# A hybrid decoder layer on one Trainium2 core: low parts of weight tiles made on VectorE in place of GpSimd, and one set of modulation shifts summed by TensorE

## The chip, the core and the metric

The kernel runs on one core of a Trainium2 chip. The core has five engines, each with an instruction queue of its own that it works through in order: TensorE (PE in the profile, with its weight loads as PEld), VectorE (DVE), ScalarE (ACT), GpSimd (POOL) and SyncE (SP, which here issues DMA transfers). The metric is device time in microseconds (us), the median over runs; less is better.

## The reference, cut to what matters

One layer for T = 512 tokens of width D = 2048, all in float32: a conditioned RMSNorm, a mixer of two groups of heads (attention with latent projections, and gated linear attention), a second conditioned RMSNorm, and a feed-forward part that picks 16 of 16,384 single-neuron experts for each token and head.

```python
c_act = silu(c)
mod = c_act @ ada_w + ada_b                       # 2048 x 12288 matrix, one vector
sh1, sc1, g1, sh2, sc2, g2 = split(mod, 6)        # shift, scale, gate, twice
h = rmsnorm(x, mix_norm_g) * (1 + sc1) + sh1
x = x + g1 * hybrid_mixer(h, ...)                 # begins with proj = h @ w_in
h = rmsnorm(x, ffn_norm_g) * (1 + sc2) + sh2
q = (h @ w_q).reshape(B, S, 8, 2, 128)            # 8 heads, 2 halves
s = einsum('bshpd,hpkd->bshpk', q, sub_keys)      # 128 keys each
top_s, top_i = top_k(s, 16)
cand = top_s[0] + top_s[1]                        # sums of pairs
best_s, best_c = top_k(cand, 16)                  # expert ids, then gates
x = x + g2 * experts(h, ids, gates)
return rmsnorm(x, final_norm_g)
```

## The kernel before

Every matrix product of float32 weights is made of three products: a weight tile is split into a high part and the rest, `whi` and `wlo`, the activations into `hhi` and `hlo` (or `h2hi`, `h2lo`), and `mm3` (L107 to 110) adds `whi·hhi`, `whi·hlo` and `wlo·hhi` in PSUM. `load_w` (L265) brings a tile by a DMA on SyncE's queue into `wraw` (five buffers in the first phase, four later) and calls `split` (L112): ScalarE copies the tile to `whi` (L115), and VectorE or GpSimd subtracts it to give `wlo` (L117). Which of the two it is, is the argument `lo_eng`.

The modulation vector is made by `mod_col` (L231). `mod_acc` brings `ada_w` in tiles of 128 x 512 elements (`adaw`, six buffers, DMA on SyncE at L222); VectorE multiplies each row by its entry of silu(c) (`cact`) and accumulates into `acc` (L226 for the first, L228 for the rest). TensorE then sums the 128 rows by a product with a column of ones (L238), and VectorE adds the bias (L240). An `adaw` tile holds four row groups of 128 columns, or one of 384 or 512: here a block of three columns of 128 takes 16 tiles of 128 x 384.

The stages that matter here, with their time in the profiled execution:

- **Start, 0 to 60 us.** Row norms of x. GpSimd scales all 16 tiles of x (L209) while VectorE makes scale A and shift B of the first block of rows (sections 1 and 0 of the modulation, by turns through `both`).
- **Blocks, 60 to 257 us.** The loop over `KBLOCKS` (L296): five blocks of 3, 3, 3, 4 and 3 tiles of 128 rows of h. For each block ScalarE makes `hhi` (L302, L303), VectorE makes `hlo` (L304), and 15 weight tiles are multiplied (L307) and added up (L314 on ScalarE in the first block, L316 on VectorE later). Between weight tiles `advance(3)` works on the modulation of the next block.
- **Gates and values, 257 to 455 us.** `gr` (L427) and `gv` (L433): 64 weight tiles of 128 x 512, with the rest of the modulation on VectorE beside them.
- **Mixer and the second norm, 455 to 907 us.** Untouched by the change, up to `h2lo` (L735) at its end.
- **Retrieval, 907 to 1104 us.** For 16 pairs of a head and a half, `w_q` tiles of 128 x 1024 (L781), products with the keys (L789), then on VectorE `top16` (L765: MAX8, FIND_INDEX8 and MATCH_REPLACE8), sums of pairs (L799), a second `top16`, and the expert ids by a one-hot compare (L820) and reduction (L826). The first expert products (`product1`, L835) fill in, with six weight tiles of their own.
- **The rest, 1104 to 3153 us.** Gates, dense expert products and the last norm. `wlo` is made on VectorE there before and after.

The order of instructions on each engine is set at build time by a scheduler that goes by the program's dependencies and its own costs; the text of the program gives it the priorities.

Of the kernel before, what the change touches and what calls it, by code (L numbers as in the profile page):

```python
# [16 lines left out]
OP = mybir.AluOpType  # L17
# [4 lines left out]
P = 128  # L22
T = 512
TB = 4
D = 2048
KD = 16
# [26 lines left out]
KBLOCKS = ((0, 3), (3, 3), (6, 3), (9, 4), (13, 3))  # L53
# [33 lines left out]
def hybrid_layer(ctx, tc, a, out):  # L87
    nc = tc.nc
# [12 lines left out]
    def bank(tag):  # L101
        return cur[tag][0].tile([P, 512], F32, name="b_" + tag, tag=tag)

    mm = nc.tensor.matmul
# [23 lines left out]
    vec = {}  # L128
# [3 lines left out]
    cact = const.tile([P, KD], F32, name="cact")  # L132
    nc.scalar.activation(cact, vec["c_t"], AF.Sigmoid)
    nc.vector.tensor_tensor(out=cact, in0=cact, in1=vec["c_t"], op=OP.mult)
    A1 = const.tile([P, KD], F32, name="A1")
    B1 = const.tile([P, KD], F32, name="B1")
# [77 lines left out]
    def ada_tile(pool):  # L214
        return pool.tile([P, 512], F32, name="adaw", tag="adaw", bufs=NADA)
# [16 lines left out]
    def mod_col(pool, sec, dst, c0, width):  # L232
        for acc in mod_acc(pool, sec, c0, width):
            yield
        b = bank("m")
        n0, nn = c0 // P, width // P
        for n in range(nn):
            mm(b[:, n:n + 1], acc[:, n * P:(n + 1) * P], ones, start=True, stop=True)  # L238
        d = dst[:, n0:n0 + nn]
        nc.vector.tensor_tensor(out=d, in0=b[:, :nn], in1=vec["ada_b_t"][:, sec * KD + n0:sec * KD + n0 + nn],  # L240
                                op=OP.add)
        if sec in (1, 4):
            g = vec["mixg"] if sec == 1 else vec["ffng"]
            nc.vector.scalar_tensor_tensor(out=d, in0=d, scalar=1.0, in1=g[:, n0:n0 + nn], op0=OP.add, op1=OP.mult)

    def mod_both(pool, c0, width):
        for acc in mod_acc(pool, 5, c0, width):
            yield
        brow = ada_tile(pool)
        nc.sync.dma_start(out=brow[0:1, :], in_=a["ada_b"][:, 5 * D + c0:5 * D + c0 + width])  # L250
        yield
        b = bank("m")
        n0, nn = c0 // P, width // P
        for n in range(nn):
            mm(b[:, n:n + 1], acc[:, n * P:(n + 1) * P], ones, start=True, stop=True)
        nc.vector.tensor_tensor(out=G2[:, n0:n0 + nn], in0=b[:, :nn],
                                in1=vec["ada_b_t"][:, 5 * KD + n0:5 * KD + n0 + nn], op=OP.add)
        b = bank("m")
        mm(b[0:1, :], ones, acc, start=True, stop=False)
        mm(b[0:1, :], ones[0:1, :], brow[0:1, :], start=False, stop=True)  # L260
        nc.scalar.copy(out=acc[0:1, :], in_=b[0:1, :])
        nc.sync.dma_start(out=g2d[:, c0:c0 + width], in_=acc[0:1, :])


    def load_w(pool, src, shape, lo_eng="vector"):  # L265
        raw = pool.tile(shape, F32, name="wraw", tag="wraw", bufs=5 if pool is wp else NWRAW)
        nc.sync.dma_start(out=raw, in_=src)
        return split(pool, raw, shape, "whi", "wlo", lo_eng=lo_eng)
# [6 lines left out]
    def both(*gens):  # L275
        gens = list(gens)
        while gens:
            for g in list(gens):
                try:
                    yield next(g)  # L280
                except StopIteration:
                    gens.remove(g)
# [9 lines left out]
    def first_mods(k0, n):  # L292
        return both(*(mod_col(ada, sec, dst, k0 * P, n * P) for sec, dst in ((1, A1), (0, B1))))

    late = first_mods(*KBLOCKS[0])
    for ib, (k0, n) in enumerate(KBLOCKS):  # L296
        for _ in late:
            pass
        late = first_mods(*KBLOCKS[ib + 1]) if ib + 1 < len(KBLOCKS) else iter(())
        for k in range(k0, k0 + n):  # L300
            t = xT[:, k, :]
            nc.scalar.activation(t, t, AF.Copy, scale=A1[:, k:k + 1])  # L302
            nc.scalar.activation(hhi[k], t, AF.Identity, bias=B1[:, k:k + 1])  # L303
            nc.vector.scalar_tensor_tensor(out=hlo[k], in0=t, scalar=B1[:, k:k + 1], in1=hhi[k],  # L304
                                           op0=OP.add, op1=OP.subtract)
        for i, dst in enumerate(dsts):
            src, m = (a["w_misc"], 80) if dst is None else (a["w_feat"][i - (i > 6)], P)  # L307
            wh, wl = load_w(wp, src[:, k0:k0 + n, :], [P, n, m], "gpsimd")
            b = bank("pj")
            for j in range(n):  # L310
                mm3(b[:m, :], wh[:, j, :], wl[:, j, :], hhi[k0 + j], hlo[k0 + j], j == 0, j == n - 1)
            for d, p in ((dst, b),) if dst is not None else ((kpe0, b[0:64, :]), (glr, b[64:80, :])):
                if ib == 0:
                    nc.scalar.copy(out=d, in_=p)  # L314
                else:
                    nc.vector.tensor_tensor(out=d, in0=p, in1=d, op=OP.add)  # L316
            advance(3)
# [24 lines left out]
    def proj_tile(pool, src, m, xh, xl, nk, evac, half=4, lo_eng="vector"):  # L342
        b = bank("pj")
        for k0 in range(0, nk, half):
            wh, wl = load_w(pool, src[:, k0:k0 + half, :], [P, half, m], lo_eng)
            for j in range(half):
                k = k0 + j
                mm3(b[:m, :], wh[:, j, :], wl[:, j, :], xh[k], xl[k], k == 0, k == nk - 1)
        evac(b)
# [4 lines left out]
    def gr_evac(i):  # L354
        def f(b):
            nc.scalar.activation(gr[:, i, :], b, AF.Sigmoid)
            nc.vector.tensor_tensor(out=gr[:, i, :], in0=b, in1=gr[:, i, :], op=OP.mult)
        return f
# [66 lines left out]
        nc.scalar.activation(cosT, ang, AF.Sin)  # L425

    for i in range(8):  # L427
        proj_tile(wp, a["w_feat"][14 + i], P, hhi, hlo, KD, gr_evac(i), lo_eng="gpsimd")
        early(i)
        advance(10)  # L430
    ckh, ckl, cqh, cql = [h[i:j] for i, j in ((0, 2), (2, 6)) for h in (hhi, hlo)]
    latents = [ckv[:, i, :] for i in range(2)] + [cq[:, i, :] for i in range(4)]
    for half in range(2):  # L433
        bs = [bank("pj") for _ in range(TB)]
        for k in range(KD):
            wh, wl = load_w(wp, a["w_gv"][half, k], [P, 512], "gpsimd")
            for tb in range(TB):
                tsl = slice(tb * P, (tb + 1) * P)
                mm3(bs[tb], hhi[k][:, tsl], hlo[k][:, tsl], wh, wl, k == 0, k == KD - 1)
            advance(2)  # L440
            if (half, k) == (0, 8):
                gates()
            if (half, k) == (0, 0):
                rotary()
            if half == 1 and k >= NLAT and latents:
                i, src = k - NLAT, latents.pop(0)
                nc.scalar.copy(out=hhi[i], in_=src)
                nc.vector.tensor_tensor(out=hlo[i], in0=src, in1=hhi[i], op=OP.subtract)
        for tb in range(TB):
            nc.scalar.copy(out=gv[:, tb, half * 512:(half + 1) * 512], in_=bs[tb])  # L450
# [58 lines left out]
    for part in range(4):  # L509
# [3 lines left out]
        for tb in range(TB):  # L513
            tsl = slice(tb * P, (tb + 1) * P)
            b = bank("up")
# [256 lines left out]
    for h in range(8):  # L772
        tv = rp.tile([P, 2, TB, 16], F32, name="tv", tag="tv")
        ti = rp.tile([P, 2, TB, 16], U32, name="ti", tag="ti")
        for p2 in range(2):
            f = h * 2 + p2
            q = rp.tile([P, T], F32, name="pq", tag="pq")
            b = bank("pj")
            b4 = b.rearrange("p (a b) -> p a b", a=NG)
            for k0 in range(0, KD, 8):  # L780
                wh, wl = load_w(ws, a["w_q"][f][:, k0:k0 + 8, :], [P, 8, P], "gpsimd")  # L781
                for j in range(8):
                    k = k0 + j
                    mm3(b4, wh[:, j, :], wl[:, j, :], h2[0][:, :, k, :], h2[1][:, :, k, :], k == 0, k == KD - 1)
            nc.scalar.copy(out=q, in_=b)
            b = bank("sk")
            for tb in range(TB):
                tsl = slice(tb * P, (tb + 1) * P)
                mm(b[:, tsl], q[:, tsl], keys[:, f, :], start=True, stop=True)  # L789
            sc = rp.tile([P, TB, P], F32, name="sc", tag="sc")  # L790
            nc.scalar.copy(out=sc, in_=b.rearrange("p (a b) -> p a b", a=TB))
            sc2 = rp.tile([P, TB, P], F32, name="sc2", tag="sc2")
            for tb in range(TB):
                top16(tv[:, p2, tb, :], ti[:, p2, tb, :], sc[:, tb, :], sc2[:, tb, :])
# [64 lines left out]
    def next1(lo_eng="vector"):  # L859
        if done1[0] - max(gated[0], NHOST) >= RAW:  # L860
            return
        j = next(todo1, None)
        if j is not None:
            for _ in product1(j, lo_eng):
                pass
            done1[0] += 1

    for _ in range(NPRE - 1):
        next1("gpsimd")
    before_exp = last_gelu[0]  # L870
    next1("gpsimd")
    nc.vector.tensor_tensor(out=gates, in0=bv, in1=bv[:, :, :, 0:1].broadcast_to([P, TB, 8, 16]), op=OP.subtract)
    after(nc.scalar.activation(gates, gates, AF.Exp), before_exp, ORDER)
    sm = rp.tile([P, TB, 8], F32, name="sm", bufs=1)
# [412 lines left out]
```

## Time and profile before

| | |
|---|---|
| median of three runs | 3154.25 us (3148.91, 3154.25, 3155.24) |
| the profiled execution, its own time | 3154.82 us |
| its span in the trace | 3153.1 us, so 1.7 us lie outside it |
| busy: PE, DVE, ACT, POOL | 96%, 81%, 35%, 26% of the span |
| mean granted TensorE clock | 0.988 |

The busy shares are means over all stages. A granted clock of 1.00 is TensorE's upper level of 2.4 GHz, and a lower mean says that part of the stretch ran at 1.2 GHz. A wait is idle time of an engine, put down to the instruction or transfer that ended it. In rows of the timeline, neighbouring instructions overlap by some 0.07 us on VectorE, so the step from one start to the next is what an instruction costs in a full queue.

### The profile page before, as it was taken

How to read it: one execution, taken by the hardware profiler on the slowest of the kernel's cores; microseconds unless marked ns; L12 is line 12 of the kernel's file. 1: busy time of each engine (PE TensorE's matmuls, PEld its weight loads, DVE VectorE, ACT ScalarE, POOL GpSimd, SP SyncE). 2: the span in 40 equal slices, each digit the busy share in tenths (PEclk: the TensorE clock that was granted, in tenths of full speed). 3: DMA queues.
4: the chain of work that ended last, by engine and by line, in shares of the span. 5: the costliest groups of instructions: out<-in, count | busy, mean ns of one | idle time of the engine just before them, and what ended most of it. 6: DMA issues, size and time to landing. Idle time of an engine off the chain costs nothing.

```text
span 3153.1 us, 46222 instructions
## 1 busy us (share of the span) xinstructions
PE 3037.6 (96%) x17617; PEld 2808.5 (89%) x17617; DVE 2563.7 (81%) x3676; ACT 1111.5 (35%) x1604; POOL 835.0 (26%) x596
## 2 busy tenths in 40 slices
PE   3988999999999999999999999999999999999997
PEld 2777777667777899999999999999999999999997
DVE  8988966677489998688888888888888888888885
ACT  3333344432232355433333333333333333333333
POOL 6445430111233300122222222222222222222210
PEclk9999998999999999999999999999999999999999
DMA  6876943038632257999999999999999999999983
GB/s 219 275 239 197 313 150 101 28 111 287 209 130 85 88 208 262 323 331 350 336 336 335 342 341 337 343 343 333 341 344 335 343 338 340 339 344 338 352 296 121
DMA packets 268527, 850.02 MB, mean 270 GB/s; under 512 B 25768, under 2 KB 99528, under 8 KB 224560
## 3 DMA queue, kind: packets, MB, share of 16 engines
q1 hardware_dynamic: 221712, 511.38, 47.4%
q0 software_dynamic: 46592, 335.68, 28.4%
q8 instruction: 138, 2.26, 0.3%
q14 instruction: 85, 0.70, 0.1%
HBM read 814.74 MB, written 32.19 MB: 269 GB/s over the span
## 4 chain that ended last, share of the span: by engine, by line
PE 84%; DVE 10%; DMA 2%; issue 2%; ACT 1%; SPq 0%; POOL 0%; ACTq 0%; DVEq 0%; POOLq 0%
PE b_p L1080 31%; PE b_p L844 21%; PE b_p L847 10%; PE b_o L703 3%; PE b_pj L109 2%; PE b_pj L110 2%; PE b_pj L108 2%; DVE acc L228 2%; PE b_gg L967 1%; DMA adaw<-in_ada_w 1%; PE b_o L108 1%; PE b_o L109 1%; PE b_o L110 1%; DVE oh L820 1%; PE b_sc L560 1%
## 5 line engine op out<-in xcount | busy, mean ns | idle before, releaser
L115 ACT CAST whi<-wraw 128x1024 fp32r<-128x1024 f32 (+2 forms) x459 | 414.2, 905 | 1036.3 <-PE b_p L844 338.4
L844 PE MATMUL b_p<-h2hi,whi 128*128 128x352 f32 x2048 | 671.4, 328 | 0.0
L844 PE MATMUL b_p<-h2lo,whi 128*128 128x352 f32 x2048 | 666.3, 326 | 0.0
L1080 PE MATMUL b_p<-h2hi,whi 128*128 128x352 f32 x2048 | 655.2, 323 | 0.6 <-DVE xo L1092 0.6
L1080 PE MATMUL b_p<-h2lo,whi 128*128 128x352 f32 x2048 | 653.8, 322 | 0.0
L1074 ACT CAST whi<-wraw 128x1024 fp32r<-128x1024 f32 x256 | 268.7, 1050 | 640.8 <-PE b_p L1080 326.5
L1075 DVE TENSOR_TENSOR wlo<-wraw,whi 128x1024 fp32r<-128x1024 f32 x256 | 312.7, 1223 | 159.6 <-ACT whi L1074 130.0
L117 DVE TENSOR_TENSOR wlo<-wraw,whi 128x1024 fp32r<-128x1024 f32 x282 | 345.0, 1224 | 65.1 <-ACT whi L115 62.0
L844 PEld LDWEIGHTS b_p<-h2lo,whi 128*128 128x128 f32 x2048 | 385.8, 188 | 0.1
L1080 PEld LDWEIGHTS b_p<-h2hi,whi 128*128 128x128 f32 x2048 | 384.4, 188 | 1.4 <-DVE xo L1092 0.9
L844 PEld LDWEIGHTS b_p<-h2hi,whi 128*128 128x128 f32 x2048 | 385.5, 188 | 0.0
L1080 PEld LDWEIGHTS b_p<-h2lo,whi 128*128 128x128 f32 x2048 | 384.9, 188 | 0.0
L228 DVE SCALAR_TENSOR_TENSOR acc<-adaw,cact,acc 128x512 f32<-128x512 f32 (+1 forms) x390 | 356.2, 932 | 29.9 <-DMA adaw<-in_ada_w 24.3
L847 PE MATMUL b_p<-h2hi,wlo 128*128 128x352 f32 x2048 | 377.9, 327 | 0.0
L1080 PE MATMUL b_p<-h2hi,wlo 128*128 128x352 f32 x2048 | 369.8, 322 | 0.0
L117 POOL TENSOR_TENSOR wlo<-wraw,whi 128x512 fp32r<-128x512 f32 (+4 forms) x177 | 277.6, 1576 | 344.5 <-ACT whi L115 333.4
L847 PEld LDWEIGHTS b_p<-h2hi,wlo 128*128 128x128 f32 x2048 | 339.1, 188 | 0.0
L1080 PEld LDWEIGHTS b_p<-h2hi,wlo 128*128 128x128 f32 x2048 | 334.0, 188 | 0.0
L995 POOL DMA_INDIRECT gat<-in_u_rows,eidx x128 | 188.3, 1471 | 510.5 <-ACT whi L1074 201.6
L995 POOL DMA_INDIRECT gat<-in_v_rows,eidx x128 | 185.5, 1449 | 515.6 <-ACT whi L1074 227.8
L1014 DVE SCALAR_TENSOR_TENSOR h2sb<-gat,wt,h2sb 128x2048 f32<-128x2048 f32 x127 | 297.9, 2346 | 26.9 <-DMA gat<-in_v_rows,eidx 26.4
L1001 DVE SCALAR_TENSOR_TENSOR gat<-gat,h2s 128x2048 f32<-128x2048 f32 x128 | 290.8, 2284 | 20.1 <-DMA gat<-in_u_rows,eidx 18.5
(375 smaller groups left out, 4194.1 us busy)
## 6 DMA issues: line engine op xcount, KB each, us to landing
wraw<-in_u_t SPq DMA_DIRECT2D x256, 512.0 KB
wraw<-in_v_t SPq DMA_DIRECT2D x256, 512.0 KB
adaw<-in_ada_w SPq DMA_DIRECT2D x288, 256.0 KB
adaw<-in_ada_w SPq DMA_DIRECT2D x128, 192.0 KB
gd<-stg SPq DMA_DIRECT2D x11, 2048.0 KB
gtile<-gd SPq DMA_DIRECT2D x32, 704.0 KB
wraw<-in_w_out SPq DMA_DIRECT2D x32, 512.0 KB
wraw<-in_w_q SPq DMA_DIRECT2D x32, 512.0 KB
```

Of the source, the lines that this page charges most:

```text
L108: mm(o, wh, xh, start=first, stop=False)
L115: nc.scalar.copy(out=hi, in_=src)
L117: last_lo[0] = e.tensor_tensor(out=lo, in0=src, in1=hi, op=OP.subtract).ins.name
L228: nc.vector.scalar_tensor_tensor(out=acc, in0=w[:, j, :], scalar=cact[:, k:k + 1], in1=acc, op0=OP.mult, op1=OP.add)
L844: mm(b3, uh[:, kk, :], x[:, GA:, k0 + kk, :], start=k0 + kk == 0 and x is h2[0], stop=False)
L847: mm(b3, ul[:, kk, :], h2[0][:, GA:, k0 + kk, :], start=False, stop=k0 + kk == KD - 1)
L995: ins = nc.gpsimd.indirect_dma_start(out=g, out_offset=None, in_=a[table], in_offset=bass.IndirectOffsetOnAxis(ap=idx[:, c:c + 1], axis=0))
L1001: after(nc.vector.scalar_tensor_tensor(out=g, in0=g, scalar=1.0, in1=of(s, h2s, h2sb)[0], op0=OP.mult, op1=OP.mult, accum_out=act0[:, s:s ...
L1014: ins = nc.vector.scalar_tensor_tensor(out=acc, in0=g, scalar=wt0[:, s:s + 1], in1=acc, op0=OP.mult, op1=OP.add)
L1074: pace[0] = nc.scalar.copy(out=vh, in_=vr).ins.name
L1075: pace[1] = nc.vector.tensor_tensor(out=vl, in0=vr, in1=vh, op=OP.subtract).ins.name
L1080: mm(banks[dc][:, :NT], part[:, jj, dc * P:(dc + 1) * P], x, start=first and jj == 0 and part is vh and x is wpair[pair * 2 + jj][0], stop ...
```

## The change

The argument "gpsimd" goes from four calls of `load_w` and `proj_tile` and from the first three `next1`, so that VectorE makes all their `wlo`: 75 tiles in the blocks, 32 in `gr`, 32 in `gv`, 32 in retrieval and 6 in the first expert products. And the shift B of the first block comes from a new function, in which TensorE multiplies the `adaw` tiles with `cact` itself: 16 tiles, three products of 128 x 128 by 128 x 1 each, summed in one bank of PSUM, and one addition on VectorE at the end.

```diff
+    def mod_pe(pool, sec, dst, c0, width):
+        b = bank("m")
+        n, kn = width // P, 512 // width
+        for k0 in range(0, KD, kn):
+            w = ada_tile(pool)[:, :kn * width].rearrange("p (k n) -> p k n", k=kn)
+            nc.sync.dma_start(out=w, in_=ada_v[:, k0:k0 + kn, sec * D + c0:sec * D + c0 + width])
+            for j in range(kn):
+                for i in range(n):
+                    mm(b[:, i:i + 1], w[:, j, i * P:(i + 1) * P], cact[:, k0 + j:k0 + j + 1],
+                       start=k0 + j + i == 0, stop=k0 + j == KD - 1 and i == n - 1)
+            yield
+        i0 = sec * KD + c0 // P
+        nc.vector.tensor_tensor(out=dst[:, c0 // P:c0 // P + n], in0=b[:, :n], in1=vec["ada_b_t"][:, i0:i0 + n], op=OP.add)
...
-    late = first_mods(*KBLOCKS[0])
+    late = both(mod_col(ada, 1, A1, 0, KBLOCKS[0][1] * P), mod_pe(ada, 0, B1, 0, KBLOCKS[0][1] * P))
...
-            wh, wl = load_w(wp, src[:, k0:k0 + n, :], [P, n, m], "gpsimd")
+            wh, wl = load_w(wp, src[:, k0:k0 + n, :], [P, n, m])
...
-        proj_tile(wp, a["w_feat"][14 + i], P, hhi, hlo, KD, gr_evac(i), lo_eng="gpsimd")
+        proj_tile(wp, a["w_feat"][14 + i], P, hhi, hlo, KD, gr_evac(i))
...
-            wh, wl = load_w(wp, a["w_gv"][half, k], [P, 512], "gpsimd")
+            wh, wl = load_w(wp, a["w_gv"][half, k], [P, 512])
...
-                wh, wl = load_w(ws, a["w_q"][f][:, k0:k0 + 8, :], [P, 8, P], "gpsimd")
+                wh, wl = load_w(ws, a["w_q"][f][:, k0:k0 + 8, :], [P, 8, P])
...
     for _ in range(NPRE - 1):
-        next1("gpsimd")
+        next1()
     before_exp = last_gelu[0]
-    next1("gpsimd")
+    next1()
```

All lines of the changed program behind the new function stand 14 further down (L304 becomes L318, L766 becomes L780). The build moves instructions; three places show how.

TensorE's queue at the start, the difference: L156 is the last product of the norm, L254 the new products, L238 the sums over rows, L108 to 110 the first weight tiles of the first block.

```order
 L156 MATMUL b_m<-ident,stat 128x128 x4
-L238 MATMUL b_m<-ones,acc 128x1 x6
-L108 MATMUL b_pj<-h0hi,whi 128x512 x2
+L254 MATMUL b_m<-cact,adaw 128x1 x48
+L238 MATMUL b_m<-ones,acc 128x1 x3
+L108 MATMUL b_pj<-h0hi,whi 128x512 x4
 L109 MATMUL b_pj<-h0lo,whi 128x512
 L110 MATMUL b_pj<-h0hi,wlo 128x512
```

The 48 new products stand between the norm's and the three sums of A; the three sums of B are gone.

VectorE's queue at the same place, the difference: L228 accumulates the modulation, L240 and L258 add the bias to A and B, L117 makes `wlo`.

```order
 L228 SCALAR_TENSOR_TENSOR acc<-adaw,cact,acc 128x384
 L151 TENSOR_TENSOR stat<-stat 128x4
-L228 SCALAR_TENSOR_TENSOR acc<-adaw,cact,acc 128x384 x21
+L117 TENSOR_TENSOR wlo<-wraw,whi 128x384 x3
+L228 SCALAR_TENSOR_TENSOR acc<-adaw,cact,acc 128x384 x11
+L258 TENSOR_TENSOR B_91<-b_m,v_ada_b_t 128x3
 L240 TENSOR_TENSOR A_90<-b_m,v_ada_b_t 128x3
```

Behind the last step of the norm (L151), 11 accumulations are left of 21, and three `wlo` stand ahead of them (a fourth stands two rows higher).

VectorE's queue where retrieval begins, before: L735 makes `h2lo`, L766 is the first MAX8 of the first `top16`.

```order
L731 SCALAR_TENSOR_TENSOR h2t<-x1T,A_92,b_m 128x512
L735 SCALAR_TENSOR_TENSOR h2lo<-h2t,B_93,h2hi 128x16x32 x2
L766 MAX tv<-sc 128x8 x2
L767 MAX_INDEX ti<-tv,sc 128x8
L768 MATCH_REPLACE sc_7532<-tv,sc 128x128
```

The same place after, and behind it the piece some 35 rows on at the sums of pairs of head 0 (L813, before L799).

```order
L745 SCALAR_TENSOR_TENSOR h2t<-x1T,A_92,b_m 128x512
L749 SCALAR_TENSOR_TENSOR h2lo<-h2t,B_93,h2hi 128x16x32
L117 TENSOR_TENSOR wlo<-wraw,whi 128x1024
L749 SCALAR_TENSOR_TENSOR h2lo<-h2t,B_93,h2hi 128x16x32
L117 TENSOR_TENSOR wlo<-wraw,whi 128x1024 x3
L780 MAX tv<-sc 128x8 x2
...
L813 TENSOR_TENSOR cd<-tv 128x4x48
L783 MAX tv<-sc_7651 128x8
L117 TENSOR_TENSOR wlo<-wraw,whi 128x1024
L784 MAX_INDEX ti<-tv,sc_7651 128x8
L813 TENSOR_TENSOR cd<-tv 128x4x64
```

Of the 38 `wlo` of 128 x 1024 that come to VectorE, seven stand ahead of the first MAX8 (three of them still further up than these rows), and 31 stand between the steps of retrieval, about four to a head, in the one queue that also holds `top16`.

## Rows read from the trace of the kernel before

**Rows 1.** Busy time by stretch (us): PE, PEld, DVE, ACT, POOL; PEclk; DMA share; GB/s.

```profile
58.00:257.00 199.00, 182.41 (x777) 142.25 (x778) 175.65 (x243) 70.98 (x130) 97.94 (x80) 0.97 0.82 257
257.00:455.00 198.00, 191.57 (x864) 156.63 (x863) 159.62 (x178) 71.06 (x111) 92.54 (x64) 0.97 0.64 211
907.00:1104.00 197.00, 194.02 (x923) 159.57 (x922) 194.24 (x897) 57.29 (x74) 74.00 (x31) 1.00 0.26 87
```

**Rows 2.** Chain of waits over the retrieval, 907 to 1104 us, by line.

```profile
by line: DVE oh L820 12.1%; DVE ti L770 9.3%; DVE ids L826 9.2%; DVE ti L767 8.6%; DVE sc L768 8.5%; DVE cd L799 6.6%; DVE tv L769 6.6%; DVE tv L766 6.4%; DVE oh L823 4.9%; DVE place L770 4.4%; DVE cd L768 4.0%; DVE place L767 4.0%; DVE pla
```

**Rows 3.** Timeline of GpSimd, then of VectorE, in head 0: start, length, what.

```profile
917.04 2.36 POOL L117 TENSOR_TENSOR wlo<-wraw,whi 128x1024 fp32r<-128x1024 f32 x1 [3.31 <-ACT whi L115]
...
916.42 0.35 DVE L799 TENSOR_TENSOR cd<-tv 128x192 f32<-128x192 f32 x1
...
917.29 2.40 DVE L799 TENSOR_TENSOR cd<-tv 128x256 f32<-128x256 f32 x1
```

**Rows 4.** Waits of TensorE, 58 to 257 us: total, times, longest.

```profile
PE b_m L238 <- DVE acc L228: 6.0, 2, 5.5
PE b_pj L110 <- POOL wlo L117: 5.2, 9, 1.7
```

**Rows 5.** Wait of TensorE, 880 to 1112 us.

```profile
PE b_pj L109 <- DVE h2lo L735: 1.8, 1, 1.8
```

**Rows 6.** Timeline of the start: TensorE (two rows), VectorE, GpSimd.

```profile
29.80 2.05 PE L156 MATMUL b_m<-ident,stat 128*128 128x128 f32 x8 [5.94 <-DVE stat L151]
...
55.87 2.95 PE L238 MATMUL b_m<-ones,acc 128*128 128x1 f32 x12 [24.02 <-DVE acc L228]
...
32.71 24.55 DVE L228 SCALAR_TENSOR_TENSOR acc<-adaw,cact,acc 128x384 f32<-128x384 f32 x16 [0.41 <-DMA adaw<-in_ada_w]
...
32.55 24.30 POOL L209 TENSOR_TENSOR xT<-xT,rr 128x512 f32<-128x512 f32 x16 [4.78 <-ACT rr L206]
```

**Rows 7.** Lines by shape, VectorE then GpSimd, 58 to 257 us: busy, mean ns.

```profile
L228 DVE SCALAR_TENSOR_TENSOR acc<-adaw,cact,acc 128x384 f32<-128x384 f32 x90 | 68.3, 808 | 5.0 <-DMA adaw<-in_ada_w 4.8
...
L228 DVE SCALAR_TENSOR_TENSOR acc<-adaw,cact,acc 128x512 f32<-128x512 f32 x56 | 52.9, 965 | 1.1 <-DMA adaw<-in_ada_w 0.7
...
L304 DVE SCALAR_TENSOR_TENSOR h1lo<-xT,B,h1hi 128x512 fp32r<-128x512 f32 x10 | 10.6, 1090 | 0.0
...
L117 POOL TENSOR_TENSOR wlo<-wraw,whi 128x384 fp32r<-128x384 f32 x54 | 64.9, 1213 | 66.6 <-ACT whi L115 64.8 <-PE b_pj L109 1.8
...
L117 POOL TENSOR_TENSOR wlo<-wraw,whi 128x512 fp32r<-128x512 f32 x17 | 24.1, 1428 | 28.4 <-ACT whi L115 28.4
```

**Rows 8.** The tile adaw over the whole span: ns min/median/max.

```profile
L228 DVE SCALAR_TENSOR_TENSOR acc<-adaw,cact,acc x390: 596/752/1864, 20.7 to 820.3; 128x512 f32<-128x512 f32 x135, 128x384 f32<-128x384 f32 x60
```

**Rows 9.** Lines by shape, VectorE, 257 to 455 us.

```profile
L228 DVE SCALAR_TENSOR_TENSOR acc<-adaw,cact,acc 128x512 f32<-128x512 f32 x95 | 109.6, 1154 | 3.4 <-DMA adaw<-in_ada_w 0.6
```

**Rows 10.** Lines by shape, VectorE, 907 to 1104 us.

```profile
L820 DVE TENSOR_TENSOR oh<-pick,iota 128x1024 bf16<-128x1024 bf16 x16 | 25.2, 1574 | 0.0
...
L799 DVE TENSOR_TENSOR cd<-tv 128x192 f32<-128x192 f32 x8 | 7.5, 940 | 0.0
...
L806 DVE TENSOR_SCALAR place<-place 128x64 uint32<-128x64 uint32 x16 | 6.9, 472 | 0.2
...
L799 DVE TENSOR_TENSOR cd<-tv 128x256 f32<-128x256 f32 x8 | 6.8, 853 | 0.0
```

**Rows 11.** Two lines by source, 907 to 1104 us: ns min/median/max.

```profile
L820 DVE TENSOR_TENSOR oh<-pick,iota x16: 676/686/2772, 927.2 to 1101.5; 128x1024 bf16<-128x1024 bf16 x16
...
L806 DVE TENSOR_SCALAR place<-place x16: 179/188/1271, 924.9 to 1098.0; 128x64 uint32<-128x64 uint32 x16
```

**Rows 12.** Timeline of VectorE at low parts that it makes before, two places.

```profile
1114.80 1.22 DVE L117 TENSOR_TENSOR wlo<-wraw,whi 128x1024 fp32r<-128x1024 f32 x1
...
1115.93 0.68 DVE L955 TENSOR_TENSOR o<-iota,slot 128x1024 f16<-128x1024 f16 x1
...
469.19 0.68 DVE L117 TENSOR_TENSOR ulo<-uraw,uhi 128x512 fp32r<-128x512 f32 x1
```

## The prediction

> **What bounds the kernel now.** I read the busy time by stretch first, since the shares of the whole span say nothing of a single stage [rows 1]. From 1104 us on the program is the same before and after, so the end moves by what the stages up to there gain or lose. In the blocks (58 to 257 us) TensorE is busy 182.4 of 199 us, VectorE 175.7, GpSimd 97.9. In the gates and values (198 us) TensorE has 191.6, VectorE 159.6, GpSimd 92.5. In retrieval (197 us) VectorE has 194.2 and TensorE 194.0, so both are full, and the chain of waits there names VectorE alone, one-hot compare (L820) first [rows 2].
>
> Then I looked at why VectorE's instructions take so long where GpSimd works beside them. In head 0 GpSimd's subtraction for a `wlo` of 128 x 1024 runs from 917.04 to 919.40 us; a sum of pairs (L799) on VectorE begins at 917.29 and ends at 919.69, 2.40 us for 256 elements a row, where one of 192 elements just before took 0.35 [rows 3]. So some instructions of VectorE stand still until GpSimd's ends. The compare at L820 shows the same: 0.69 us at the median, 2.77 at most; L806 0.19 and 1.27 [rows 11]. The Trainium skill, page "SBUF — State Buffer", section "Who interferes with whom", says that VectorE's second pair of ports is GpSimd's only one, held as an exclusive lock by whichever uses it; the trace agrees with the 2.40 us beside 0.35. By that rule the whole excess goes when GpSimd falls silent, as in the sum below; without it the same sum would have 27 us more in retrieval.
>
> Last I read what TensorE waits for. In the blocks the largest are 6.0 us for the modulation's accumulation (one wait of 5.5) and 5.2 us in nine waits for a `wlo` of GpSimd [rows 4]. Ahead of retrieval there is one of 1.8 us for `h2lo` [rows 5].
>
> **The start.** TensorE ends the norm's spread at 31.85 us and then waits 24.0 us for VectorE's accumulation [rows 6]. VectorE runs 16 accumulations there in 24.55 us, 1.53 each, beside GpSimd's 16 scalings in 24.30. The change takes the shift's 16 accumulations from VectorE and gives TensorE 48 products. The nearest row is the sums at L238, of the same shape (128 x 128 by 128 x 1): 12 instructions for six calls in 2.95 us, 0.246 each. So 48 calls are 96 instructions, 23.6 us, and they stand behind the norm in the queue: 31.85 + 23.6 = 55.5, and three sums of A (six instructions, 1.5 us) end at 57.0. On VectorE 11 accumulations and three or four `wlo` at 1.53 each, since GpSimd's scaling still runs, take 21 to 23 us from 32.7 on, so its end is 54 to 56 us, too. Before, the sums of A were done at 57.3 and those of B at 58.8. TensorE's wait is thus filled with work of nearly the same length: **0**. The bounds: if the products took no time the start would come at VectorE's 55 + 1.5, hardly a gain; without the lock VectorE's 14 or 15 instructions of about 0.6 would be through some 14 us sooner, but then TensorE's 23.6 hold. If a product costs 0.2 instead of 0.246 and the accumulations slip between the scalings, some 4 to 6 us are gained. To lose, the transfers have to be late: a `wlo` now stands in VectorE's queue ahead of accumulations and waits for ScalarE's copy and the tile's DMA, and the shift's tiles hold `adaw` buffers until TensorE is past the norm. The same queue showed 0.41 us of waiting for transfers [rows 6], so I bound this by +3.
>
> **The blocks.** GpSimd loses 54 `wlo` of 128 x 384, 17 of 128 x 512 and five smaller ones in this stretch [rows 7]. On VectorE a `wlo` of 128 x 1024 lasts 1.22 us and the next instruction starts 1.13 after it; one of 128 x 512 lasts 0.68, so its step is about 0.60 [rows 12]; in a line between them 128 x 384 is 0.47 (an estimate). That is 25.4 + 10.2 + 1.7 = 37.3 us more. What VectorE gets back: the accumulation's lowest and median durations over all are 0.596 (384) and 0.752 (512) [rows 8], against means of 0.808 x 90 and 0.965 x 56 here [rows 7], so 19.1 + 11.9, and `h1lo` 10 x (1.090 - 0.752) = 3.4: 34.4 us. VectorE's load hardly changes (+3 on 175.7 of 199). TensorE's 5.2 us of waits for GpSimd's slow subtraction (1.2 us each) are answered by one of 0.5, but in a queue that has evacuations and accumulations ahead of it. I take half of these waits as gone: **-3**. The bounds are 0, and all that the two waits hold, -11.
>
> **Gates and values.** 64 `wlo` of 128 x 512 come to VectorE, 38 us at 0.60; the 95 accumulations have a mean of 1.154 [rows 9] against 0.752, so 38 us are given back. TensorE is busy 191.6 of 198 and VectorE has 38 us of slack that cover an error: **0**, with 6 either way, which is what TensorE leaves idle.
>
> **Before retrieval.** The wait of 1.8 us for `h2lo` [rows 5] was the end of a stretch in which GpSimd already made the first `wlo` of `w_q`; now these stand between or behind the `h2lo` in the same queue, so a little over one subtraction is in front: **-2** (bounds -3 and +2).
>
> **Retrieval.** Of the 38 tiles, 31 stand among the steps of the heads: 31 x 1.13 = 35.0 us. Given back: L820 16 x (1.574 - 0.686) = 14.2, L799 8 x (0.940 - 0.35) + 8 x (0.853 - 0.42) = 8.2 (0.42 for 256 elements is an estimate from 0.35 for 192), L806 16 x (0.472 - 0.188) = 4.5 [rows 3, 10, 11], together 26.9. VectorE comes to 194.2 + 8.1 = 202.3 us in a stretch of 197, so it sets the length. As it kept 2.8 us of idle before, I take **+8**; if that idle goes, +5.
>
> The sum: 0 - 3 + 0 - 2 + 8 = +3 on the profiled execution's 3154.8 us. Its own time is 0.6 above the median of the three runs, so the median should come to 3157. A change of 0.2% (6.3 us) is about what a measurement of this kernel can tell from none.
>
> **The rivals.** *Slower: VectorE's one queue.* In retrieval a `wlo` waits for ScalarE's copy, and `top16`, which is ready, stands behind it; TensorE in turn waits for a `wlo` that stands behind `top16` of an earlier half. 0.5 us at each of 31 places would be 15.5, 3172. The other form: VectorE's and TensorE's steps were matched before (194.2 and 194.0 us), so part of the excess in L820 and L799 was slack that VectorE had to wait away in any case; if half of the 26.9 is not got back, the end is 13.5 later, 3171. It decides as soon as VectorE carries more than 3 us beyond TensorE's 194. Against it stands that the chain of waits shows nothing but VectorE [rows 2], so the excess was real there.
>
> *Faster: TensorE alone sets the blocks.* If the `wlo` now come early enough, both waits of [rows 4] go (11.2 us), and with the long one the lower clock behind it: a mean of 0.97 over 199 us [rows 1] is 6 us of work not done. That is 14 more than my -3, so 3143; with half of it 3150. For it speaks that most of what VectorE waits for there are transfers of `adaw` [rows 7], with load left; against it, that VectorE's load does not fall, and that the 5.5 us were a wait for VectorE.
>
> *The change does not do what it says at the start, or does more.* That the start comes no sooner is my forecast. If the products are quicker than the row says, and VectorE's accumulations also, 6 us come out: 3151, or up to 3145.
>
> **How the numbers follow.** The forecast has 0.42, with a range of its own of 3150 to 3164 (0.34 within 0.2%, 0.08 slower). The slower rival has 0.28, since the one queue has to serve TensorE's weights and the bounding chain at once, and lies between 3165 and 3178. The faster one has 0.20 (0.19 faster, 0.01 the same), the early start 0.10 (half faster, half the same). So faster 0.24, same 0.40, slower 0.36. The range 3143 to 3174 reaches to the middle of both sides and takes in the bounds: 3 + 6 + 5 below by start, values and blocks, and 15 above by the queue.
>
> **What the changed profile would show.** GpSimd silent behind 60 us except for its few other lines. L820 (there L834) at 0.69 us in all 16 instructions, L799 (L813) under 0.45, the accumulation at 0.60 and 0.75. TensorE's products of the shift from about 31.9 to 55.5 us, and its first weight product at 60, not before 57. In retrieval VectorE without idle time, with its chain longer by 5 to 8 us, and TensorE with waits for `wlo` of VectorE that add up to as much. I am wrong if these waits exceed 15 us, if the blocks end over 8 us earlier, or if VectorE's steps do not shrink to their lowest durations.

## The result, and the profile after

The changed kernel takes 3130.09 us (median of four runs, 3125.52 to 3131.46) against 3154.63 us before: 0.9926 of the time, 95% interval 0.9912 to 0.9941. That is 24.5 us faster and below the stated range of 3143 to 3174. The profiled execution has 3131.46 us with a span of 3129.8, against 3154.82 and 3153.1.

Where the span's 23.3 us went is read from the start of the same instruction in both traces:

| from, to | before (us) | after | change | predicted |
|---|---|---|---|---|
| 0, first weight product of the blocks | 60.0 | 55.3 | -4.7 | 0 |
| to the first product of `gr` (blocks) | 196.9 | 184.3 | -12.6 | -3 |
| to the first output product of the mixer (`b_ob`, L582; gates and values lie here) | 295.8 | 289.1 | -6.7 | 0 |
| to the first MAX8 of `top16` | 354.8 | 351.0 | -3.8 | -2 |
| to the last operation on the gates (L877; retrieval) | 198.3 | 201.4 | +3.1 | +8 |
| to the end | 2047.3 | 2048.7 | +1.4 | 0 |

Every term came out lower than predicted but for the last. Busy time by stretch, in the columns of [rows 1], with the blocks, the stage up to the mixer's output, and retrieval between just these instructions, first before, then after:

```profile
59.98:256.93 196.95, 181.51 (x773) 141.44 (x773) 174.47 (x240) 69.00 (x127) 97.93 (x79) 0.97 0.82 258
256.93:552.74 295.81, 284.67 (x1286) 226.26 (x1285) 224.80 (x311) 124.85 (x222) 96.53 (x73) 0.94 0.57 185
907.50:1105.80 198.30, 194.93 (x929) 160.30 (x927) 195.97 (x903) 57.55 (x75) 74.00 (x31) 1.00 0.26 86
```

```profile
55.33:239.62 184.29, 178.47 (x772) 139.26 (x773) 173.30 (x309) 68.33 (x126) 6.07 (x4) 1.00 0.84 265
239.62:528.69 289.07, 281.94 (x1286) 224.50 (x1284) 211.02 (x376) 124.50 (x221) 4.62 (x11) 0.96 0.59 192
879.70:1081.10 201.40, 196.41 (x925) 161.36 (x923) 199.99 (x930) 56.94 (x73) 0.00 (x0) 0.99 0.26 84
```

GpSimd is all but silent. In the blocks VectorE is as busy as before (173.3 us; 174.5 before in the same stretch), but the stretch is 12.6 us shorter. So it is VectorE's idle time that fell: from 22.5 us to 11.0. TensorE's idle time fell from 15.4 us to 5.8, and its busy time from 181.5 to 178.5. Here is what VectorE waited for in the blocks, first before, then after (total, times, longest):

```profile
DVE acc L226 <- DMA adaw<-in_ada_w: 8.3, 2, 7.7
DVE acc L228 <- DMA adaw<-in_ada_w: 5.5, 7, 2.2
```

```profile
DVE wlo L117 <- ACT whi L115: 2.8, 5, 0.9
DVE gk L330 <- PE b_pj L110: 2.8, 4, 1.0
...
DVE acc L228 <- DMA adaw<-in_ada_w: 1.4, 4, 0.5
```

13.8 us of waiting for modulation tiles became 1.4. TensorE's waits of [rows 4] went with it; this is the same view after:

```profile
PE b_pj L108 <- ACT whi L115: 3.9, 9, 0.9
PE b_pj L108 <- ACT h0hi L317: 2.9, 1, 2.9
PE b_pj L110 <- DVE wlo L117: 1.1, 4, 0.3
```

The two largest entries, 6.0 us for the accumulation and 5.2 for GpSimd's `wlo`, are gone, and the clock granted in the blocks is 1.00 where it was 0.97.

VectorE's instructions fell to about their lowest durations, as forecast. By shape in the blocks, and in retrieval:

```profile
L228 DVE SCALAR_TENSOR_TENSOR acc<-adaw,cact,acc 128x384 f32<-128x384 f32 x88 | 50.4, 614 | 1.5 <-DMA adaw<-in_ada_w 1.4
L228 DVE SCALAR_TENSOR_TENSOR acc<-adaw,cact,acc 128x512 f32<-128x512 f32 x49 | 36.1, 768 | 0.1
L117 DVE TENSOR_TENSOR wlo<-wraw,whi 128x384 fp32r<-128x384 f32 x52 | 28.8, 561 | 2.8 <-ACT whi L115 2.8
...
L117 DVE TENSOR_TENSOR wlo<-wraw,whi 128x512 fp32r<-128x512 f32 x16 | 10.8, 686 | 0.0
```

```profile
L117 DVE TENSOR_TENSOR wlo<-wraw,whi 128x1024 fp32r<-128x1024 f32 x31 | 37.7, 1215 | 0.2 <-ACT whi L115 0.2
...
L834 DVE TENSOR_TENSOR oh<-pick,iota 128x1024 bf16<-128x1024 bf16 x16 | 11.0, 684 | 0.0
...
L813 DVE TENSOR_TENSOR cd<-tv 128x256 f32<-128x256 f32 x8 | 3.3, 407 | 0.0
...
L813 DVE TENSOR_TENSOR cd<-tv 128x192 f32<-128x192 f32 x8 | 2.8, 354 | 0.0
...
L820 DVE TENSOR_SCALAR place<-place 128x64 uint32<-128x64 uint32 x16 | 2.3, 192 | 0.0
```

The compare is at 684 ns (1574 in [rows 10]), the accumulations at 614 and 768 (808 and 965 in [rows 7]).

The start is read in two places. On VectorE, the last step of the norm (L151), before and after:

```profile
23.98 2.94 DVE L228 SCALAR_TENSOR_TENSOR acc<-adaw,cact,acc 128x384 f32<-128x384 f32 x4
...
26.93 1.25 DVE L228 SCALAR_TENSOR_TENSOR acc<-adaw,cact,acc 128x384 f32<-128x384 f32 x1
...
28.18 0.60 DVE L228 SCALAR_TENSOR_TENSOR acc<-adaw,cact,acc 128x384 f32<-128x384 f32 x1
...
28.97 0.61 DVE L228 SCALAR_TENSOR_TENSOR acc<-adaw,cact,acc 128x384 f32<-128x384 f32 x1
29.50 0.15 DVE L151 TENSOR_TENSOR stat<-stat 128x4 f32<-128x4 f32 x1
```

```profile
23.56 0.62 DVE L228 SCALAR_TENSOR_TENSOR acc<-adaw,cact,acc 128x384 f32<-128x384 f32 x1
...
25.12 0.61 DVE L228 SCALAR_TENSOR_TENSOR acc<-adaw,cact,acc 128x384 f32<-128x384 f32 x1
25.65 0.16 DVE L151 TENSOR_TENSOR stat<-stat 128x4 f32<-128x4 f32 x1
```

And TensorE's queue after:

```profile
25.95 2.04 PE L156 MATMUL b_m<-ident,stat 128*128 128x128 f32 x8 [2.51 <-DVE stat L151]
27.79 10.33 PE L254 MATMUL b_m<-cact,adaw 128*128 128x1 f32 x48
...
51.02 1.41 PE L238 MATMUL b_m<-ones,acc 128*128 128x1 f32 x6
55.33 2.08 PE L108 MATMUL b_pj<-h0hi,whi 128*128 128x512 f32 x4 [2.89 <-ACT h0hi L317]
```

Before, seven accumulations of the scale and the shift stood between the small steps of the norm; after, two of the scale and one `wlo`. L151 comes 3.9 us sooner. TensorE's products begin at 27.8 instead of the 31.85 of my sum, and 48 instructions take 10.33 us, 0.215 each instead of 0.246.

### The profile page after: what moved, and what is told of

The parts are those of the page before. It is cut to its first block, busy times and chain, and to the rows that moved or that the text cites. A ratio compares the mean times of both kernels' runs of the same rounds, so it can differ in the third digit from the quotient of the medians.

```text
span 3129.8 us, 46257 instructions
## 1 busy us (share of the span) xinstructions
PE 3052.6 (98%) x17707; PEld 2824.2 (90%) x17707; DVE 2542.2 (81%) x3837; ACT 1111.5 (36%) x1603; POOL 576.0 (18%) x419
## 4 chain that ended last, share of the span: by engine, by line
PE 91%; DVE 5%; DMA 2%; issue 1%; ACT 1%; ACTq 0%; SPq 0%; DVEq 0%
PE b_p L1094 31%; PE b_p L858 21%; PE b_p L861 10%; PE b_pj L110 4%; PE b_pj L108 4%; PE b_pj L109 4%; PE b_o L717 3%; PE b_gg L981 1%; DMA adaw<-in_ada_w 1%; PE b_o L108 1%; PE b_o L109 1%; PE b_o L110 1%; DVE acc L228 1%; DVE wlo L117 1%; PE b_sc L574 1%
## 5 line engine op out<-in xcount | busy, mean ns | idle before, releaser
L117 DVE TENSOR_TENSOR wlo<-wraw,whi 128x1024 fp32r<-128x1024 f32 (+2 forms) x459 | 479.3, 1047 | 103.2 <-ACT whi L115 100.1
L1089 DVE TENSOR_TENSOR wlo<-wraw,whi 128x1024 fp32r<-128x1024 f32 x256 | 313.7, 1226 | 162.4 <-ACT whi L1088 133.1
L228 DVE SCALAR_TENSOR_TENSOR acc<-adaw,cact,acc 128x512 f32<-128x512 f32 (+1 forms) x375 | 271.9, 740 | 42.3 <-DMA adaw<-in_ada_w 38.3
L1009 POOL DMA_INDIRECT gat<-in_u_rows,eidx x128 | 198.9, 1554 | 496.9 <-ACT whi L1088 208.4
L1106 DVE TENSOR_TENSOR xo<-b_p,xo 128x352 f32<-128x352 f32 x236 | 107.3, 518 | 64.5 <-PE b_p L1094 64.4
```

The source lines that it names most:

```text
L117: last_lo[0] = e.tensor_tensor(out=lo, in0=src, in1=hi, op=OP.subtract).ins.name
L228: nc.vector.scalar_tensor_tensor(out=acc, in0=w[:, j, :], scalar=cact[:, k:k + 1], in1=acc, op0=OP.mult, op1=OP.add)
L1009: ins = nc.gpsimd.indirect_dma_start(out=g, out_offset=None, in_=a[table], in_offset=bass.IndirectOffsetOnAxis(ap=idx[:, c:c + 1], axis=0))
L1089: pace[1] = nc.vector.tensor_tensor(out=vl, in0=vr, in1=vh, op=OP.subtract).ins.name
```

## The experiments

The first four take the change apart. In the diffs, lines with + are what the kernel has against the kernel named.

**The start alone**, against before:

```diff
-    late = first_mods(*KBLOCKS[0])
+    late = both(mod_col(ada, 1, A1, 0, KBLOCKS[0][1] * P), mod_pe(ada, 0, B1, 0, KBLOCKS[0][1] * P))
```

> Only the first block's shift is summed by TensorE; every low part is made by GpSimd as before. Theory (each stage gains by itself): the first weight product of the blocks comes 4 to 5 us sooner, as in the changed kernel (55.3 instead of 60.0 us), the blocks take as long as before (197 us from first to last product), and the time falls by 4 to 5 us to about 3150. Rival (the earlier start gives the blocks their lead): the blocks are shorter as well, and the time falls by 10 us or more.

Measured 0.9979 of before (0.9968 to 0.9990), 6 to 7 us. The first weight product comes at 56.9 us, 3.1 us sooner, and the blocks take 197.4 us (VectorE 176.8 busy). The rival falls: the start does not shorten the blocks.

**The blocks alone**, against before:

```diff
-            wh, wl = load_w(wp, src[:, k0:k0 + n, :], [P, n, m], "gpsimd")
+            wh, wl = load_w(wp, src[:, k0:k0 + n, :], [P, n, m])
```

> Only the 75 low parts of the blocks are made by VectorE; the start, the gates and values and retrieval are as before. Theory (TensorE no longer waits for GpSimd's slow subtraction and for accumulations that stood still beside it): the blocks take 184 to 186 us instead of 197, the time falls by 11 to 13 us to about 3142. Rival (the blocks gain because of the earlier start): they gain 3 us or less, the time is about 3151.

Measured 0.9973 (0.9961 to 0.9986), 8 to 9 us; the blocks take 186.6 us, and VectorE is busy for 174.7 of them. The gain in the blocks is that of their own low parts.

**Gates and values alone**: the argument "gpsimd" goes from `gr` and `gv`.

> Only the 64 low parts of gates and values are made by VectorE. Theory (the 6.4 us that TensorE waits for the latent norm at 276 us come from a wait of VectorE for the positions' transfer, which the changed program issues elsewhere, not from the low parts): the gain is there only if that wait goes; with the order of before at this place it stays and the time is within 2 us of 3154.6. Rival (the low parts hold this stage back): 5 to 7 us faster, about 3148.

Measured 0.9995 (0.9985 to 1.0005): no gain. TensorE's wait for the latent norm is 3.6 us here (6.4 before), though VectorE's wait for the positions is still there, 6.6 us.

**Retrieval alone**: the argument goes from `w_q` and `next1`.

> Only the 38 low parts of w_q and of the first expert products are made by VectorE. Theory: ahead of retrieval 3 to 4 us are gained and in retrieval 4 lost, so the time is within 2 us of 3154.6. Rival (the prediction's +8 in retrieval and -2 ahead of it): 6 us slower, about 3160.

Measured 0.9988 (0.9979 to 0.9998), 3 to 4 us faster, more than the theory had: 350.9 us instead of 354.8 up to the first MAX8, and 200.8 instead of 198.3 in retrieval. The prediction's +8 is refuted. The four ratios add up to -0.65%, the whole change has -0.74%.

**Only the first low parts of retrieval on VectorE**, against the changed kernel:

```diff
-                wh, wl = load_w(ws, a["w_q"][f][:, k0:k0 + 8, :], [P, 8, P])
+                wh, wl = load_w(ws, a["w_q"][f][:, k0:k0 + 8, :], [P, 8, P], "vector" if f < 4 else "gpsimd")
...
-        next1()
+        next1("gpsimd")
```

> The changed kernel, but only the first four of the 16 pairs of a head and a half have their low parts of w_q made by VectorE (8 tiles); the other 24 tiles and the six of the first expert products go back to GpSimd. Theory (the low parts that stand ahead of the first top-16 gain 3 to 4 us, those between the heads lose 3 to 4): another 2 to 4 us faster than the changed kernel's 3130, and retrieval from the first MAX8 to the gates takes 198 to 199 us instead of 201. Rival (GpSimd's lock costs VectorE as much as the low parts do): the same as the changed kernel within 1 us.

Measured 3125.63 us, 0.9914 (0.9898 to 0.9931): the fastest version, though its interval overlaps that of the changed kernel, so that the gain over it is not shown. Up to the first MAX8 it takes 349.4 us, and retrieval 199.7.

**A low part that nobody reads**, against the changed kernel. In the blocks GpSimd makes the same subtraction a second time; the copy holds the tile's buffers until it is done, and in the program nothing else changes:

```diff
+        if ghost:
+            g = pool.tile(shape, F32, name="ghost", tag="ghost", bufs=1)
+            nc.gpsimd.tensor_tensor(out=g, in0=src, in1=hi, op=OP.subtract)
...
-            wh, wl = load_w(wp, src[:, k0:k0 + n, :], [P, n, m])
+            wh, wl = load_w(wp, src[:, k0:k0 + n, :], [P, n, m], ghost=True)
```

> The changed kernel, with a second copy of each low part of the blocks that GpSimd makes and nobody reads: VectorE still makes the low part that is used. This brings back GpSimd's hold on VectorE (and on the tile's buffers), but not TensorE's wait for a slow subtraction. Theory 1 (the hold, since VectorE is full in this stage): the accumulations go back to means of 0.8 to 1.0 us and the blocks, 184 us in the changed kernel, take 20 to 30 us longer, about 3155. Theory 2 (TensorE's waits for GpSimd's result): the blocks stay within 4 us of the changed kernel, about 3132.

Measured 3167.71 us, 1.0048 of before (1.0031 to 1.0065). The blocks by stretch, what TensorE waits for, and three groups of VectorE:

```profile
56.50:273.85 217.35, 184.03 (x772) 138.00 (x773) 209.30 (x306) 67.63 (x125) 91.46 (x75) 1.00 0.72 223
```

```profile
PE b_pj L110 <- DVE wlo L117: 28.6, 27, 3.0
```

```profile
L231 DVE SCALAR_TENSOR_TENSOR acc<-adaw,cact,acc 128x384 f32<-128x384 f32 x90 | 65.9, 772 | 1.6 <-DMA adaw<-in_ada_w 1.6
L231 DVE SCALAR_TENSOR_TENSOR acc<-adaw,cact,acc 128x512 f32<-128x512 f32 x50 | 42.2, 875 | 0.1
L117 DVE TENSOR_TENSOR wlo<-wraw,whi 128x384 fp32r<-128x384 f32 x52 | 39.2, 764 | 2.1 <-ACT whi L115 2.1
```

The blocks take 33 us longer. VectorE's busy time rises by 36.0 us with no more to do, and TensorE waits for it. So GpSimd's hold on VectorE costs what it seems to cost, and in this version VectorE sets the length of the stage.

**Every other tile**, against before: the blocks' `load_w` gets ("vector", "gpsimd")[i % 2].

> The kernel before, with every other tile of the blocks (the even ones of the 15) on VectorE, the rest on GpSimd; start, values and retrieval as before. Theory 1 (what matters is how much VectorE stands still): half of the 10 us that the blocks alone gained, so 3147 to 3149. Theory 2 (what matters is where the queues put the late pieces: the one wait of 5.5 us for the shift's accumulation and the 7.7 us that VectorE waits for a tile behind six weight transfers): all or nothing, 3142 or 3153, according to whether these two waits are there.

Measured 1.0003 (0.9993 to 1.0012). Both theories miss. The two waits of the second theory are gone, TensorE's for the accumulation and VectorE's of 7.7 us for a tile, but the blocks take 196.9 us as before; VectorE is busy 177.9 and waits 7.8 us for modulation tiles, and TensorE waits as in this row:

```profile
PE b_pj L110 <- DVE wlo L117: 12.8, 12, 3.3
```

VectorE has the new low parts and still stands behind the other 35 of GpSimd; half the way gains nothing.

**Scale and shift of the first block by TensorE**, against the changed kernel:

```diff
+        if sec == 1:
+            d = dst[:, c0 // P:c0 // P + n]
...
-    late = both(mod_col(ada, 1, A1, 0, KBLOCKS[0][1] * P), mod_pe(ada, 0, B1, 0, KBLOCKS[0][1] * P))
+    late = both(mod_pe(ada, 1, A1, 0, KBLOCKS[0][1] * P), mod_pe(ada, 0, B1, 0, KBLOCKS[0][1] * P))
```

> The changed kernel with the first block's scale summed by TensorE too: 96 products instead of 48, and no accumulation on VectorE at the start. Theory (at the start TensorE's products, 0.222 us an instruction, are what the first block waits for): the first weight product comes 21 us later than in the changed kernel, at 76 us instead of 55.3, and the time rises by 15 to 21 us to about 3148. Rival (VectorE beside GpSimd, or the transfers, set the start): it comes at most 5 us later, and the time is about 3130 to 3135.

Measured 3144.64 us, 0.9977 (0.9967 to 0.9987). TensorE's queue at the start:

```profile
27.22 40.96 PE L254 MATMUL b_m<-cact,adaw 128*128 128x1 f32 x192
69.39 2.08 PE L108 MATMUL b_pj<-h0hi,whi 128*128 128x512 f32 x4 [1.21 <-ACT h0hi L320]
```

192 instructions in 40.96 us, 0.213 each and without a pause; the first block comes 14 us later, less than the 21 expected: no product waits for a transfer, the sums at L238 fall away, and the wait for `h0hi` is 1.21 us instead of 2.89. TensorE's products do set the start once they are this many.

**The modulation tiles from ScalarE's queue**, in blocks 1 to 4, once against before, once against the changed kernel, and once in the version with the first low parts of retrieval only:

```diff
+    adaq = [nc.sync]
...
-            nc.sync.dma_start(out=w, in_=ada_v[:, k0:k0 + kn, sec * D + c0:sec * D + c0 + width])
+            adaq[0].dma_start(out=w, in_=ada_v[:, k0:k0 + kn, sec * D + c0:sec * D + c0 + width])
...
+        adaq[0] = nc.scalar
...
+    adaq[0] = nc.sync
```

> The kernel before, with GpSimd's low parts, but the modulation tiles of blocks 1 to 4 are issued from ScalarE's queue instead of SyncE's, so that they no longer stand behind weight tiles whose buffers GpSimd frees late. Theory (the blocks gained because these tiles came in time: VectorE waited 13.8 us for them before, 1.4 after): VectorE's waits for them fall under 5 us and the blocks take 186 to 190 us instead of 197, about 3144. Rival (VectorE is full with its work and GpSimd's hold, and the waits for transfers are only where its lost time shows): the waits go or not, the blocks stay over 194 us, about 3152.

> The changed kernel with the same move of the modulation tiles to ScalarE's queue. Theory and rival agree that little is left to win there (VectorE waits 1.4 us for them): within 3 us of the changed kernel; more waits of TensorE for ScalarE's copies, whose queue now holds the issues.

> Both: the low parts of the first four pairs alone on VectorE in retrieval, and the modulation tiles from ScalarE's queue. If the two effects are separate, the time is that of the first alone (3125.6) plus what the queue gives beside the changed kernel.

Measured 1.0080 (1.0064 to 1.0097), 0.9969 (0.9960 to 0.9979) and 0.9968 (0.9953 to 0.9983). The first two expectations miss: the tiles came later, not sooner (the blocks take 219.9 us in the first). The third holds within 2 us (3139.78; the parts give 3125.63 and the 12.2 that the queue costs the changed kernel, 3137.8). In the second one, this is what VectorE and ScalarE waited for:

```profile
DVE acc L230 <- DMA adaw<-in_ada_w: 10.8, 13, 2.5
```

```profile
ACT whi L115 <- DVE acc L230: 27.5, 11, 4.0
```

VectorE's load is 174.2 us, as before and after; its waits for the tiles go from 1.4 to 10.8 us, and the blocks from 184.3 to 197.8 us, about the length before the change. But ScalarE's copies now stand behind issues that wait until an accumulation has freed an `adaw` buffer (27.5 us, 0.3 in the changed kernel), and TensorE waits 11.3 us for `wlo` of VectorE. So it is not shown what late tiles alone cost.

**The changed kernel on the chip of these last three:**

> The changed kernel itself on the chip of these runs, so that the versions are compared on one chip: 0.9926 of the time before (0.991 to 0.994).

Measured 3129.26 us, 0.9936 (0.9919 to 0.9953); here the stage up to the mixer's output takes 284.1 us, where the first execution had 289.1.

**One more buffer**, against before, for the modulation tiles (NADA = 7) and for the weight tiles of the first phase (six `wraw` instead of five):

> The kernel before with seven adaw buffers instead of six, low parts on GpSimd. If VectorE's lost time in the blocks (22.5 us idle, 13.8 of it waiting for modulation tiles) comes from too few tiles in flight, these waits fall under 8 us and the blocks take 190 us or less instead of 197, about 3147. If the tiles are late because SyncE stands at a weight tile's buffer, which GpSimd has not freed, one more adaw buffer changes the blocks by less than 3 us, about 3152.

> The kernel before with six wraw buffers instead of five in the first phase, low parts on GpSimd. If SyncE's 19 us of waiting for buffers that GpSimd frees late is what holds up the modulation tiles behind them, those waits fall below 10 us, VectorE's waits for the tiles below 8 us, and the blocks to 190 us or less, about 3147. If the queue's order, or VectorE standing still behind GpSimd, is the cause, the blocks stay within 3 us of 197, about 3152.

Measured 0.9986 (0.9976 to 0.9997) and 1.0001 (0.9991 to 1.0011); the blocks take 196.0 and 194.8 us. VectorE still waits 9.4 and 13.0 us for tiles. One more buffer of either kind is not enough to bring them in time.

## Why the prediction was wrong

**The blocks**, 9.6 of the 26.3 us between the sum's +3 and the -23.3 of the trace. The step that failed is "I take half of these waits as gone: -3". Both entries of [rows 4] went whole, and the low clock with them; the -12.6 lie beyond even the bound of -11. The blocks' own low parts did it: they alone brought -10.3.

I sized the stage by TensorE's waits, and used VectorE only to see that its load does not change. It did not (174.5 and 173.3 us; the sum had +3). But the prediction uses the chain of waits for retrieval alone. In the blocks it is this, before and after, in shares of the stretch ("issue" is time in which an engine waited for nothing that the profile shows):

```profile
by line: DVE acc L228 18.0%; issue 17.6%; DMA adaw<-in_ada_w 14.7%; PE b_pj L110 6.3%; PE b_pj L109 6.0%; DMA wraw<-in_w_feat 5.7%; PE b_pj L108 5.5%; DVE h1lo L304 5.2%; POOL wlo L117 2.7%; DMA wraw<-in_w_misc 2.6%; DVE cq L316 2.6%; PE b_
```

```profile
by line: PE b_pj L110 17.4%; PE b_pj L108 16.9%; PE b_pj L109 15.9%; DMA adaw<-in_ada_w 15.3%; DVE acc L228 10.4%; issue 5.9%; DVE wlo L117 5.4%; DMA wraw<-in_w_feat 4.1%; PE b_m L238 2.9%; DMA wraw<-in_w_misc 1.4%; DVE gk L330 0.8%; DVE gl
```

Before, VectorE's accumulations have the largest share, 18.0%, the transfers of their tiles 14.7%, and TensorE's products at L108 to 110 together 17.8%; after, these products have 50.2%. So before, the length came more from VectorE's work and the transfers than from TensorE, whose waits I had read. Over the kernels (busy and idle time of VectorE add up to the length in every row; what tells is which of the two moves):

| kernel | blocks | VectorE busy | idle | of it for `adaw` |
|---|---|---|---|---|
| before | 196.9 | 174.5 | 22.5 | 13.8 |
| the start alone | 197.4 | 176.8 | 20.6 | 12.7 |
| every other tile | 196.9 | 177.9 | 19.0 | 7.8 |
| the blocks alone | 186.6 | 174.7 | 11.9 | 1.3 |
| changed | 184.3 | 173.3 | 11.0 | 1.4 |
| changed, `adaw` from ScalarE | 197.8 | 174.2 | 23.6 | 10.8 |
| changed, unread copies | 217.4 | 209.3 | 8.0 | 2.4 |

Low parts on VectorE cost it as much as GpSimd's hold had cost, and what was gained is idle time; its waits for modulation tiles fell with it. That late tiles were the cause is not shown: with every other tile these waits fell to 7.8 us, with seven `adaw` buffers to 9.4, and the blocks still took 196.9 and 196.0 us. The faster rival had the outcome in this stage (all waits of [rows 4] and the low clock gone), with a chance of 0.20; it put the clock at 6 us, and TensorE's busy time fell by 3.0. Its mechanism, TensorE alone, is not enough: with every other tile both entries of [rows 4] are gone as well, and 12.8 us of waits for VectorE's `wlo` stand in their place.

Why the tiles came late before is not settled. In the trace before, the longest such wait ends at 218 us (the second row), behind this piece of SyncE's queue:

```profile
201.63 8.14 SPq L267 DMA_DIRECT2D wraw<-in_w_feat  x6
209.82 0.42 SPq L476 DMA_DIRECT2D uraw<-in_w_ukn  x1
```

```profile
218.41 0.49 DVE L226 TENSOR_SCALAR acc<-adaw,cact 128x512 f32<-128x512 f32 x1 [7.74 <-DMA adaw<-in_ada_w]
```

Six weight tiles and then tiles of a later stage were issued ahead of the next modulation tiles, and between 195 and 222 us SyncE waited 4.1 us for buffers that GpSimd's `wlo` still held. That this order, made at build time, is the cause is only argued: one more buffer of either kind took at most 2.1 us off the blocks, and the order by itself was not changed.

**The start** (0 forecast, -4.7). The step that failed is "they stand behind the norm in the queue: 31.85 + 23.6 = 55.5": the norm itself ends sooner. The accumulations taken away had also stood between its steps, which I did not use; 4 us come from that (27.8 instead of 31.85). The cheaper products, 0.215 us instead of 0.246 for an instruction at first, brought little: with five short waits for transfers among them (1.9 us) the 96 take 23.2 us, where the sum had 23.6. The bound of "4 to 6 us" had the size by luck, since it rested on cheaper products.

**Gates and values** (0 with 6 either way, -6.7). The bound nearly covers it, but no step of mine does, and the cause stays open. TensorE's wait for the latent norm, before, after, and with the blocks' low parts alone on VectorE:

```profile
PE b_m L156 <- DVE stat L151: 6.4, 1, 6.4
```

```profile
PE b_m L156 <- DVE stat L151: 1.3, 1, 1.3
```

```profile
PE b_m L156 <- DVE stat L151: 7.3, 1, 7.3
```

Before, VectorE stood for the transfer of the positions ahead of the norm's last steps:

```profile
271.06 0.43 DVE L396 CAST ang<-posi 128x512 f32<-128x512 int32 x1 [4.94 <-DMA posi<-in_positions]
```

After, it does not wait for them. But with the blocks' low parts alone it does not either, and TensorE's wait is 7.3 us all the same, so the positions do not explain it. The mean granted clock from the blocks' end to the mixer's output rose from 0.94 to 0.96. The change of `gr` and `gv` alone did not bring the gain. One kernel, run twice, differs by 5 us here (289.1 and 284.1), and the eight kernels whose gates and values are made as before range from 289.0 to 297.3 us; the 289.1 lie inside that range, so the -6.7 cannot be told from the spread of single executions.

**Before retrieval** (-2, got -3.8): the right way, and too small. TensorE's wait for `h2lo` is 1.0 us instead of 1.8, and the one of 0.8 for GpSimd is gone; the rest was not traced to a cause.

**Retrieval** (+8, got +3.1). The mechanism held: VectorE is busy 200.0 of 201.4 us and sets the length. The sum had its load rise by 8.1 us; it rose by 4.0. From one start to the next the 31 `wlo` take 35.0 us, the figure of the sum, and the three groups give back 14.4, 8.4 and 4.6, against 14.2, 8.2 and 4.5. The mis-sized term is what I left out: MAX8, FIND_INDEX8 and MATCH_REPLACE8 got shorter steps too, 3.6 us in all, and the rest is small pieces. The slower rival shows in one place only, a wait of TensorE of 1.9 us for a `wlo` at 906 us.

With GpSimd silent there, no excess is left in L834 (684 ns), L813 (407 and 354) or L820 (192). This agrees with the Trainium skill, page "SBUF — State Buffer", section "Who interferes with whom", by which the two engines share a pair of ports that one of them holds at a time.

## What to carry to other kernels

Ask of each stage through which engine the chain of waits runs, and then what that engine's idle time waits for: an exchange of load that comes out even can still win. Where an engine works beside one that holds it up, count the hold as its work. Half a move need not bring half the gain; here it brought nothing. When instructions are taken out of a queue, look at what stood between and behind them, not only at what they were for.

## What was not expected of the hardware

75 subtractions by GpSimd that nobody reads cost VectorE 36.0 us of busy time and the blocks 33 us, more than the 20 to 30 expected. An operation with one tensor and constants (L806, 128 x 64 elements) was held as well, as the prediction had counted: 472 ns on average beside GpSimd, 192 without. A product of 128 x 128 by 128 x 1 on TensorE took 0.213 us an instruction in a row of 192, 0.246 in the twelve of [rows 6].
